# A hybrid decoder layer on one core: the delta rule's low-rank products change places with the first block of its input projections

## The chip, the core and the metric

The kernel runs on one core of a Trainium2 chip. The core has a matrix engine (TensorE, PE in the profile; PEld is its loading of weights), a vector engine (VectorE, DVE), a scalar engine (ScalarE, ACT), GpSimd (POOL) and a queue that only issues transfers (SyncE, SP). The metric is the device time of one execution in microseconds; lower is better.

## What is computed

One layer of a decoder trunk over 256 tokens of width 2048, in float32. Three token mixers (an mLSTM, an RWKV-7 delta rule, an S5 state space) read one combined projection of the normalised input. Their outputs are gated and merged, and a SwiGLU and a gated embedding follow. What this change touches is the front of the delta rule:

```python
z = xn @ w_in                      # columns: mLSTM | RWKV-7 | S5 | three gates
r, kr, vr, wl, al, gl = jnp.split(_token_shift(zr, mu), RWKV_SPLIT, axis=-1)
w = -softplus(-(w0 + jnp.tanh(wl) @ w2)) - 0.5     # w2: 96 x 512
a = sigmoid(a0 + al @ a2)                          # a2: 96 x 512
g = sigmoid(gl) @ g2                               # g2: 256 x 512
# r, kr, vr: 512 columns each; w, a, g enter the recurrence over 256 steps
```

Beside it in the program stands the S5 mixer: a complex diagonal recurrence, computed in eight slices of 2 x 128 states.

## The kernel before

**Weights.** Every weight matrix is cut into chunks of 512 x 512 (1 MB). The host lays them out one behind the other in the order of use (`layout`, array `wall`), and the kernel takes them strictly in that order: `load` issues the next chunk on SP into `raw` (a ring of three), `chunk` splits it, half a chunk at a time, into a high part `whi` (a cast on ACT, L124) and a low part `wlo` (a subtraction on DVE, L125). Each of these rings has three buffers of half a chunk. A product in full precision then takes three matmuls: high by high, high by low, low by high.

**Products.** A large product is a `gemm_fm` (weights stationary, L145, L146, L148) or a `gemm_tm` (activations stationary, L138, L139, L141). Each takes four chunks and two PSUM banks of the pool `mm`, which has four banks. `fm_small` (L131 to L133) is the small form; `lora` calls it three times on one chunk, with two banks each time and 12, 12 and 24 matmuls.

**The stages that the change touches.** `z_lora`, early in the program, computes the low-rank columns into `zpL`, which stays in SBUF. Much later `lora` makes the operands of the second product from it: the token shift into `lx` (ACT and DVE), tanh, then the split into `Lh` (a cast on ACT) and `Ll` (a subtraction on DVE); then it takes its chunk and runs the three small products, whose results ACT reads out into the tiles `lora`. `z_rkv(i)` for i = 0, 1, 2 computes r, k and v: a `gemm_fm`, read out of PSUM by DVE into `zp`, then a token shift on ACT and DVE into `mur`, `muk`, `muv`. `s5_slice(ip, jj)` begins with four matmuls on the tile `ub` (L489), then a long row of DVE work (`xr_`, `xi_`, `sr`, `si`, `wa`, `rr`), and every second slice a product with `cc` (L535). The tile `ub` has one buffer, which six transfers on POOL (L473, L474) refill for the next slice once the four matmuls have read it. The last part of the mLSTM, `ml_out`, scales `oth` on DVE and transposes it on PE (L356).

**Buffers.** `lx`, `Lh`, `Ll`, the three `lora` tiles, `zp`, `mur` and many others are tiles of 128 x 1024 from one pool (`t4`, 12 buffers). PSUM for the smaller products is the pool `sm` (four banks).

**What sets the order.** The order of the calls at the end of `trunk` is a wish: a scheduler orders the instructions of each engine when the program is built, by its own estimate of when each can run, with the earlier call in front where several can. `chunk` and the reading of PSUM have high priority. On the chip each engine's order is then fixed. The order of the calls and the order of the chunks in `wall` must agree, since chunks are taken in turn.

Of the kernel before, what the change touches and what calls it, by code (L numbers as in the profile page):

```python
# [70 lines left out]
def trunk(ctx: ExitStack, tc: tile.TileContext, xT, x, pT, wall, vecs, csts, s5b, s5c, gfin, out, dbg=None):  # L71
# [131 lines left out]
    def ts(o, i, a, b=None, op0=ALU.mult, op1=ALU.add):  # L203
        if b is None:
            nc.vector.tensor_scalar(out=o, in0=i, scalar1=a, scalar2=None, op0=op0)
        else:
            nc.vector.tensor_scalar(out=o, in0=i, scalar1=a, scalar2=b, op0=op0, op1=op1)
# [4 lines left out]
    def stt(o, a, s, b, op0, op1):  # L212
        nc.vector.scalar_tensor_tensor(out=o, in0=a, scalar=s, in1=b, op0=op0, op1=op1)
# [19 lines left out]
    def t8(name, dt=F32):  # L233
        return mp.tile([128, 8, T], dt, name=name, tag="b8", bufs=2)
# [116 lines left out]
    def tposed(src, n0):  # L351

        pt = psm()
        for a in range(2):
            for t in range(2):
                nc.tensor.transpose(pt[:, a * 256 + t * 128:a * 256 + (t + 1) * 128], src[t][:, (n0 + a) * 128:(n0 + a + 1) * 128], ident)  # L356
        return pt
# [346 lines left out]
    def ml_out():  # L704
        num, rh, oth = G["num"], G["rh"], G["o"]
        ymh, yml = t8("ymh", F32R), t8("yml", F32R)
        for t in range(2):
            stt(oth[t], oth[t], 1.0, num[t][:, :, 0:256], ALU.add, ALU.mult)
            for h in range(4):
                ts(oth[t][:, h, :], oth[t][:, h, :], rh[:, 4 * t + h:4 * t + h + 1])  # L710
        of = [o.rearrange("p h c -> p (h c)") for o in oth]
        for q in range(4):
            pt = tposed(of, 2 * q)
            for a in range(2):
                k = 2 * q + a
                split(ymh[:, k, :], yml[:, k, :], pt[:, a * 256:(a + 1) * 256], V("mng", k))
        G.update(ymh=ymh, yml=yml)
        dump("ymh", ymh.bitcast(F32))
        dump("yml", yml.bitcast(F32))
# [24 lines left out]
    def lora():  # L744
        zpL = G["zpL"]
        Lh = t4v(4, "Lh").bitcast(F32R)
        Ll = t4v(4, "Ll").bitcast(F32R)
        lx = t4v(4, "lx")
        for f in range(4):
            act_fn(lx[:, f, :], zpL[:, f, 1:257], AF.Identity, scale=omu(12 + f))  # L750
            stt(lx[:, f, :], zpL[:, f, 0:256], V("mul", f), lx[:, f, :], ALU.mult, ALU.add)
        act_fn(lx[:, 0, :], lx[:, 0, :], AF.Tanh)
        act_fn(lx[:, 2:4, :], lx[:, 2:4, :], AF.Tanh, scale=0.5)
        ts(lx[:, 2:4, :], lx[:, 2:4, :], 0.5, 0.5)
        split(Lh, Ll, lx)
        w = chunk()
        out_ = []
        for ks in ((0,), (1,), (2, 3)):
            rows = slice(0, 96) if ks[0] < 2 else slice(0, 128)
            ps = fm_small(w, ks, rows, lambda k: Lh[:, k, :], lambda k: Ll[:, k, :])  # L760
            o = t4v(4, "lora")
            for f in range(4):
                if ks[0] < 2:
                    i = 16 + 4 * ks[0] + f
                    act_fn(o[:, f, :], quarter(ps, f), AF.Tanh, scale=0.5, bias=vd[:, i:i + 1])
                else:
                    nc.scalar.copy(out=o[:, f, :], in_=quarter(ps, f))
            out_.append(o)
        G["lw"], G["aa"], G["gF"] = out_

    def z_rkv(i):
        mu = ("mur", "muk", "muv")[i]
        ps = gemm_fm(xh, xl, NKT)
        zp = t4("zp")[:, 0:1028].rearrange("p (a t) -> p a t", a=4)
        nc.vector.memset(zp[:, :, 0:1], 0.0)
        evac_fm(ps, zp, 1)
        o = t4v(4, mu)
        for f in range(4):
            act_fn(o[:, f, :], zp[:, f, 1:257], AF.Identity, scale=omu(4 * i + f))
            stt(o[:, f, :], zp[:, f, 0:256], V(mu, f), o[:, f, :], ALU.mult, ALU.add)  # L780
        G["rkv"[i] + "F"] = o
# [319 lines left out]
    ml_num()  # L1101
    z_o(1)
    ml_out()
    lora()
    z_rkv(0)
    s5_slice(1, 0)
    z_rkv(1)
    s5_slice(1, 1)
# [185 lines left out]
def layout(i):  # L1294

    f32 = np.float32
    a = {k: np.asarray(v) for k, v in i.items()}

    def fm(v):
        return np.ascontiguousarray(v.reshape(-1, 128).T)  # L1300

    def pad(v, n):
        o = np.zeros((n,), f32)
        o[:v.shape[0]] = v
        return o

    mu = a["rwkv_mu"][0]
    mul = np.concatenate([pad(mu[1536:1632], 128), pad(mu[1632:1728], 128), mu[1728:1984]])
    ifb = np.zeros((128, 2), f32)
    ifb[96:100, 0] = a["mlstm_ib"][0]  # L1310
    ifb[96:100, 1] = a["mlstm_fb"][0]
    ldt = np.ascontiguousarray(np.broadcast_to(a["s5_log_dt"][0][:, None], (32, 64)))
    parts = {
        "gmix": fm(a["norm_mix_g"][0]), "gffn": fm(a["norm_ffn_g"][0]), "gple": fm(a["norm_ple_g"][0]),
        "mng": fm(a["mlstm_norm_g"][0]), "conv": fm(a["mlstm_conv"][0]),
        "mur": fm(mu[0:512]), "muk": fm(mu[512:1024]), "muv": fm(mu[1024:1536]), "mul": fm(mul),
        "w0": fm(a["rwkv_w0"][0]), "a0": fm(a["rwkv_a0"][0]), "kk": fm(a["rwkv_kk"][0]), "ka": fm(a["rwkv_ka"][0]),
        "rk": fm(a["rwkv_rk"][0]), "lng": fm(a["rwkv_ln_g"][0]), "lnb": fm(a["rwkv_ln_b"][0]),
        "d": fm(a["s5_d"][0]), "glub": fm(a["s5_glu_b"][0]),
        "are": fm(a["s5_a_re"][0]), "aim": fm(a["s5_a_im"][0]), "ldt": fm(ldt), "ifb": ifb,  # L1320
    }
    vecs = np.concatenate([parts[n] for n, _ in VEC], axis=1)

    w_in = a["w_in"][0]
    z28 = np.zeros((D, 28), f32)
    lora_c = np.concatenate([w_in[:, 5640:5736], w_in[:, 4096:4100], z28, w_in[:, 5736:5832], w_in[:, 4100:4104], z28, w_in[:, 5832:6088]], axis=1)

    chunks = []

    def block(w):  # L1330
        k = w.shape[0]
        for c in range(k // 512):
            chunks.append(w[c * 512:(c + 1) * 512].reshape(4, 128, 512).transpose(1, 0, 2).reshape(128, 2048))

    def blocks(w):
        for n in range(w.shape[1] // 512):
            block(w[:, n * 512:(n + 1) * 512])

    block(w_in[:, 6088:6600])
    block(lora_c)  # L1340
    blocks(w_in[:, 0:4096])
    lw = np.zeros((4, 128, 512), f32)
    lw[0, :96] = a["rwkv_w2"][0]
    lw[1, :96] = a["rwkv_a2"][0]
    lw[2:4] = a["rwkv_g2"][0].reshape(2, 128, 512)
    block(lw.reshape(512, 512))
    blocks(w_in[:, 4104:5640])
    blocks(w_in[:, 6600:8648])
    block(a["s5_glu_w"][0])
    blocks(a["w_up_m"][0])  # L1350
    for n in range(4):
        block(w_in[:, 10696 + n * 512:10696 + (n + 1) * 512])
        block(a["w_up_s"][0][:, n * 512:(n + 1) * 512])
    blocks(w_in[:, 8648:10696])
    blocks(a["w_up_r"][0])
    blocks(a["w_out"][0])
    for n in range(11):
        block(a["ffn_w_gate"][0][:, n * 512:(n + 1) * 512])
        block(a["ffn_w_up"][0][:, n * 512:(n + 1) * 512])
    blocks(a["ffn_w_down"][0])  # L1360
    wp = a["ple_w_proj"][0]
    for n in range(4):
        if n % 2 == 0:
            block(np.concatenate([wp[:, n * 512:(n + 1) * 512], wp[:, (n + 1) * 512:(n + 2) * 512]], axis=0))
        block(a["ple_w_gate"][0][:, n * 512:(n + 1) * 512])
    wall = np.stack(chunks)

    s5b = np.zeros((128, 4, 2, 128), f32)
    s5c = np.zeros((128, 2, 16, 32), f32)
    for ri, (nb, ncn) in enumerate((("s5_b_re", "s5_c_re"), ("s5_b_im", "s5_c_im"))):  # L1370
        b, c = a[nb][0], a[ncn][0]
        for g in range(32):
            i_, jj, gg = g // 8, (g % 8) // 2, g % 2
            s5b[32 * jj + 16 * gg:32 * jj + 16 * gg + 16, i_, ri, 64 * gg:64 * gg + 64] = b[g].T
            s5c[64 * gg:64 * gg + 64, ri, g // 2, 16 * gg:16 * gg + 16] = c[g].T
    x2 = a["x"][0]
    return {
        "xT": np.ascontiguousarray(x2.T.reshape(16, 128, T).transpose(1, 0, 2)),
        "x": np.ascontiguousarray(x2),
        "pT": np.ascontiguousarray(a["p"][0, 0].T.reshape(2, 128, T).transpose(1, 0, 2)),  # L1380
        "wall": wall,
        "vecs": vecs,
        "csts": shape_constants(),
        "s5b": s5b,
        "s5c": s5c.reshape(128, 2, 512),
        "gfin": np.ascontiguousarray(a["final_norm_g"].reshape(1, D)),
    }
# [17 lines left out]
```

## Time and profile before

| | before |
|---|---|
| median of 3 runs | 1680.63 us (1679.04 to 1680.68) |
| the profiled execution, its own time | 1679.8 us |
| span of the profile (first to last instruction) | 1678.0 us |
| PE busy | 1658.7 us (99%) |
| DVE busy | 1059.9 us (63%) |
| ACT busy | 808.0 us (48%) |
| mean granted clock of TensorE | 0.998 of full speed |

The span is what the rows below are read from; the profiled execution took 1.8 us more than its span, and is 0.8 us under the median. A busy share is an average: what a stage is worth has to be read in that stage. Matmuls are pipelined, so the time from one start to the next says more than the duration of one.

### The profile page before, as it was taken

To read this page: it belongs to the slowest core of one execution; us is meant where nothing else is said; L and a number is where in the kernel's file an instruction comes from. 1 tells how busy PE (TensorE), PEld (TensorE's weight loads), DVE (VectorE), ACT (ScalarE), POOL (GpSimd) and SP (SyncE) were. 2 spreads that over 40 slices of the span, in tenths; PEclk is the share of its full clock that TensorE was granted. 3 is DMA by queue.
4 is the path that set the end of the run, shared out by engine and by line. 5 is a ranking of instruction groups with operands and counts; after the bars stand their busy time and mean duration, and the time that the engine had idled before them with its cause. 6 is when DMAs were issued, how large, how long until landed. Compare 5 with 4: busy or idle time off the path is not lost.

```text
span 1678.0 us, 22986 instructions
## 1 busy us (share of the span) xinstructions
PE 1658.7 (99%) x9354; PEld 1403.3 (84%) x9354; DVE 1059.9 (63%) x1330; ACT 808.0 (48%) x995; POOL 42.4 (3%) x65
## 2 busy tenths in 40 slices
PE   8999999999999999999999999999999999999997
PEld 8998889987888878888888888888888888888886
DVE  7999776968987555575555555555555545544565
ACT  6465566455555434444444444444444434444444
POOL 1100100100000000000000000000000000000000
PEclk9999999999999999999999999999999999999999
DMA  9654544555454444556555555555555555555553
GB/s 361 196 182 175 172 154 176 187 188 181 176 182 151 148 152 153 197 188 209 203 186 198 179 197 183 194 187 189 191 185 195 183 198 185 192 197 181 221 185 120
DMA packets 49450, 313.66 MB, mean 187 GB/s; under 512 B 5824, under 2 KB 9152, under 8 KB 12736
## 3 DMA queue, kind: packets, MB, share of 16 engines
q1 hardware_dynamic: 43488, 304.59, 50.7%
q0 software_dynamic: 3840, 3.15, 1.1%
q10 hardware_dynamic: 2016, 4.46, 0.8%
q8 instruction: 73, 1.20, 0.3%
q14 instruction: 33, 0.27, 0.0%
HBM read 306.93 MB, written 2.10 MB: 184 GB/s over the span
## 4 chain that ended last, share of the span: by engine, by line
PE 98%; ACT 1%; issue 1%; DMA 0%; DVE 0%; SPq 0%; POOLq 0%; POOL 0%
PE mm L138 26%; PE mm L139 26%; PE mm L141 26%; PE mm L145 4%; PE mm L146 4%; PE mm L148 4%; PE sm L535 1%; PE sm L1213 1%; PE mm L132 0%; PE mm L131 0%; PE mm L133 0%; PE sm L1158 0%; PE sm L878 0%; PE sm L356 0%; PE sm L1014 0%
## 5 line engine op out<-in xcount | busy, mean ns | idle before, releaser
L125 DVE TENSOR_TENSOR wlo<-raw,whi 128x1024 fp32r<-128x1024 f32 (+1 forms) x562 | 683.6, 1218 | 505.7 <-ACT whi L124 464.3
L124 ACT CAST whi<-raw 128x1024 fp32r<-128x1024 f32 (+1 forms) x562 | 589.1, 1049 | 788.1 <-PE mm L139 666.8
L138 PE MATMUL mm<-whi,hhi 128*128 128x512 f32 x704 | 274.1, 389 | 0.0
L139 PE MATMUL mm<-whi,hlo 128*128 128x512 f32 x704 | 274.0, 389 | 0.0
L139 PE MATMUL mm<-whi,alo 128*128 128x512 f32 x512 | 201.2, 393 | 0.0
L138 PE MATMUL mm<-whi,ahi 128*128 128x512 f32 x512 | 201.0, 393 | 0.0
L141 PE MATMUL mm<-wlo,hhi 128*128 128x512 f32 x704 | 193.5, 392 | 0.0
L139 PEld LDWEIGHTS mm<-whi,hlo 128*128 128x128 f32 x704 | 132.2, 188 | 27.6
L138 PEld LDWEIGHTS mm<-whi,hhi 128*128 128x128 f32 x704 | 132.2, 188 | 27.2
L141 PEld LDWEIGHTS mm<-wlo,hhi 128*128 128x128 f32 x704 | 132.2, 188 | 26.6
L145 PE MATMUL mm<-ahi,whi 128*128 128x256 f32 x576 | 143.2, 286 | 7.2 <-ACT whi L124 7.2
L146 PE MATMUL mm<-alo,whi 128*128 128x256 f32 x576 | 142.9, 285 | 0.0
L141 PE MATMUL mm<-wlo,ahi 128*128 128x512 f32 x512 | 139.3, 392 | 0.0
L138 PE MATMUL mm<-whi,gh 128*128 128x512 f32 x352 | 137.0, 389 | 0.0
L139 PE MATMUL mm<-whi,gl 128*128 128x512 f32 x352 | 137.0, 389 | 0.0
L145 PEld LDWEIGHTS mm<-ahi,whi 128*128 128x128 f32 x576 | 111.4, 194 | 8.0 <-ACT whi L124 7.2
L138 PEld LDWEIGHTS mm<-whi,ahi 128*128 128x128 f32 x512 | 96.1, 188 | 21.2 <-issue 1.2
L139 PEld LDWEIGHTS mm<-whi,alo 128*128 128x128 f32 x512 | 96.1, 188 | 21.0 <-issue 1.2
L141 PEld LDWEIGHTS mm<-wlo,ahi 128*128 128x128 f32 x512 | 95.6, 188 | 20.6 <-issue 0.4
L146 PEld LDWEIGHTS mm<-alo,whi 128*128 128x128 f32 x576 | 111.5, 194 | 0.4 <-issue 0.4
L141 PE MATMUL mm<-wlo,gh 128*128 128x512 f32 x352 | 96.0, 391 | 0.0
L148 PE MATMUL mm<-ahi,wlo 128*128 128x256 f32 x576 | 81.7, 284 | 0.0
(493 smaller groups left out, 1888.9 us busy)
## 6 DMA issues: line engine op xcount, KB each, us to landing
raw<-in_wall SPq DMA_DIRECT2D x283, 1024.0 KB, 4.8
xrow<-in_x SPq DMA_DIRECT2D x2, 1024.0 KB, 9.6
h<-in_x ACTq DMA_DIRECT2D x8, 256.0 KB, 3.3
xraw<-in_xT SPq DMA_DIRECT2D x3, 512.0 KB, 10.0
ub<-Bh POOLq DMA_DIRECT2D x16, 64.0 KB, 4.2
ub<-uh POOLq DMA_DIRECT2D x16, 64.0 KB, 4.4
gft<-in_gfin ACTq DMA_DIRECT2D x1, 1024.0 KB, 7.3
out_dram<-fin SPq DMA_DIRECT2D x4, 256.0 KB, 3.2
```

The costliest lines, as they stand in the source:

```text
L124: nc.scalar.copy(out=hi[:, q, :], in_=r)
L125: nc.vector.tensor_tensor(out=lo[:, q, :], in0=r, in1=hi[:, q, :].bitcast(F32), op=ALU.subtract)
L138: nc.tensor.matmul(ps, ah, wh, start=first, stop=False, skip_group_check=skip)
L139: nc.tensor.matmul(ps, al, wh, start=False, stop=False, skip_group_check=skip)
L141: nc.tensor.matmul(ps, ah, wl, start=False, stop=last, skip_group_check=skip)
L145: nc.tensor.matmul(ps, wh, ah, start=first, stop=False, skip_group_check=skip)
L146: nc.tensor.matmul(ps, wh, al, start=False, stop=False, skip_group_check=skip)
L148: nc.tensor.matmul(ps, wl, ah, start=False, stop=last, skip_group_check=skip)
L535: nc.tensor.matmul(psy[32 * j:32 * j + 32, a * 256:(a + 1) * 256], cc[:, ri, js_, :], G["s5x"][q][ri][:, a, :], start=ri == 0, stop=ri == ...
L1213: nc.tensor.transpose(pt[:, a * 256 + t * 128:a * 256 + (t + 1) * 128], sg[t][:, (2 * q + a) * 128:(2 * q + a + 1) * 128], ident)
```

## The change

In the list of calls, `lora()` moves behind `z_rkv(0)`, and in `layout` its chunk of weights moves behind the four chunks of `z_rkv(0)`:

```diff
     ml_num()
     z_o(1)
     ml_out()
+    z_rkv(0)
     lora()
-    z_rkv(0)
     s5_slice(1, 0)
     z_rkv(1)
...
     blocks(w_in[:, 0:4096])
+    blocks(w_in[:, 4104:4616])
     lw = np.zeros((4, 128, 512), f32)
...
     block(lw.reshape(512, 512))
-    blocks(w_in[:, 4104:5640])
+    blocks(w_in[:, 4616:5640])
     blocks(w_in[:, 6600:8648])
```

No instruction is added or removed. The scheduler, however, orders the neighbourhood anew, on three engines. In the rows of order below, the numbers are those of buffers.

**PE, where the three small products of `lora` begin.** Before, they stand right behind the last matmuls of `z_o(1)` (L141):

```order
L141 MATMUL mm_2564<-wlo_2675,ahi_82 128x512
L141 MATMUL mm_2565<-wlo_2675,ahi_82 128x512
L131 MATMUL mm_2778<-Lh_2752,whi_2770 128x256
L132 MATMUL mm_2778<-Ll_2753,whi_2770 128x256
L133 MATMUL mm_2778<-Lh_2752,wlo_2771 128x256
```

In the change they stand behind the last matmuls of `z_rkv(0)` (L148), with eight matmuls of S5 between (L489): four on `ub_2302`, which belong to `s5_slice(1, 0)`, and four on `ub_3101`, which belong to `s5_slice(1, 1)`:

```order
L148 MATMUL mm_2753<-ahi_82,wlo_2935 128x256 x2
L489 MATMUL sm_3095<-ub_2302 128x256
L489 MATMUL sm_3096<-ub_2302 128x256
L489 MATMUL sm_3095<-ub_2302 128x256
L489 MATMUL sm_3096<-ub_2302 128x256
L489 MATMUL sm_3392<-ub_3101 128x256
L489 MATMUL sm_3393<-ub_3101 128x256
L489 MATMUL sm_3392<-ub_3101 128x256
L489 MATMUL sm_3393<-ub_3101 128x256
L131 MATMUL mm_3025<-Lh_2999,whi_3017 128x256
```

Before, the four on `ub_3101` stood behind `z_rkv(1)`, a whole block of 192 matmuls after the four on `ub_2302`. Behind the first L131 of the change stand three more L131 and then the first L132, which reads `Ll`.

**ACT, where the operands of `lora` are made.** Before, the token shift `lx` stands among the casts of `z_o(1)`'s weights and the copies of `ml_num` (`num`, `jk`), far ahead of `z_rkv(0)`:

```order
L216 ACTIVATE oth_2359<-mm_2361,hrs0_398 128x512
L688 COPY num_2500<-sm_2504 128x258
L688 COPY num_2501<-sm_2510 128x258
L688 COPY num_2500<-sm_2517 128x258
L216 ACTIVATE lx_2754<-zpL_431,vd_140 128x256 x4
L216 ACTIVATE jk_2507,nss_2502<-num_2500 128x256
L124 CAST whi_2606<-raw_2600 128x1024
```

In the change it stands behind the cast for `z_rkv(1)`'s first weights, and behind the first two rows of `mur`, which read the result of `z_rkv(0)` from `zp`:

```order
L124 CAST whi_3149<-raw_3147 128x1024
L216 ACTIVATE mur_2990<-zp_2986,vd_140 128x256 x2
L216 ACTIVATE lx_3001<-zpL_431,vd_140 128x256 x4
L216 ACTIVATE mur_2990<-zp_2986,vd_140 128x256 x2
L216 ACTIVATE lx_3001<-lx_3001 128x256
L216 ACTIVATE lx_3001<-lx_3001 128x512
L184 CAST Lh_2999<-lx_3001 128x1024
```

**DVE, the same place.** Before, the three rows of `lora`'s operands stand between subtractions of weights (`wlo`), far ahead of `z_rkv(0)`:

```order
L213 SCALAR_TENSOR_TENSOR lx_2754<-zpL_431,vt_73,lx_2754 128x256 x4
L125 TENSOR_TENSOR wlo_2607<-raw_2600,whi_2606 128x1024
L207 TENSOR_SCALAR lx_2754<-lx_2754 128x512
L125 TENSOR_TENSOR wlo_2637<-raw_2634,whi_2636 128x1024
L185 TENSOR_TENSOR Ll_2753<-lx_2754,Lh_2752 128x1024
```

In the change they stand behind the reading of `z_rkv(0)`'s banks (two rows of `zp`, one `wlo`, then four rows of 128x512 that read `s5_slice(1, 0)`'s banks, all ahead of this piece) and among the rest of that slice's work:

```order
L213 SCALAR_TENSOR_TENSOR mur_2990<-zp_2986,vt_73,mur_2990 128x256 x2
L213 SCALAR_TENSOR_TENSOR lx_3001<-zpL_431,vt_73,lx_3001 128x256 x4
L213 SCALAR_TENSOR_TENSOR mur_2990<-zp_2986,vt_73,mur_2990 128x256 x2
L210 TENSOR_TENSOR xr__3125<-xr__3125,wa_3109 128x512
L210 TENSOR_TENSOR xi__3126<-xi__3126,rr_3108 128x512
L207 TENSOR_SCALAR lx_3001<-lx_3001 128x512
L519 SCALAR_TENSOR_TENSOR sr_3133<-s16mag_670,xr__3125 128x256 x2
L519 SCALAR_TENSOR_TENSOR si_3134<-s16mag_670,xi__3126 128x256 x2
L207 TENSOR_SCALAR wa_3406<-trow_663,s16f_681 128x256 x2
L210 TENSOR_TENSOR xr__3125<-sr_3133,tc_3110 128x512
L210 TENSOR_TENSOR rr_3108<-sr_3133,tsn_3111 128x512
L185 TENSOR_TENSOR Ll_3000<-lx_3001,Lh_2999 128x1024
```

What moved, beside the products: the making of their operands now begins behind `z_rkv(0)` instead of ahead of it. The rows of SP and POOL are in the same order in both programs.

## Rows read from the trace of the kernel before

**Rows 1.** The page: the span, and the chain that ended last.

```profile
span 1678.0 us, 22986 instructions
PE 98%; ACT 1%; issue 1%; DMA 0%; DVE 0%; SPq 0%; POOLq 0%; POOL 0%
```

**Rows 2.** PE's two longest waits: us in total, times, longest.

```profile
PE mm L145 <- ACT whi L124: 7.2, 1, 7.2
PE mm L131 <- ACT oth L216: 1.6, 1, 1.6
```

**Rows 3.** Timeline of PE through `lora`: start, us, instruction, count, idle before.

```profile
257.13 0.28 PE L131 MATMUL mm<-Lh,whi 96*128 96x256 f32 x1
...
260.25 0.41 PE L131 MATMUL mm<-Lh,whi 96*128 96x256 f32 x1 [1.59 <-ACT oth L216]
...
264.01 0.28 PE L131 MATMUL mm<-Lh,whi 128*128 128x256 f32 x1
...
266.05 0.28 PE L145 MATMUL mm<-ahi,whi 128*128 128x256 f32 x1
```

**Rows 4.** Windows of that stretch: busy PE, PEld, DVE, ACT, POOL, then PEclk.

```profile
257.00:258.70 1.70, 1.67 (x14) 1.43 (x12) 1.46 (x2) 1.68 (x3) 0.00 (x0) 1.00 0.00 0
262.00:263.00 1.00, 1.00 (x6) 1.00 (x6) 1.00 (x3) 1.00 (x4) 0.00 (x0) 0.50 0.14 57
```

**Rows 5.** Timeline of ACT and DVE: the operands of `lora` before.

```profile
235.38 1.74 ACT L216 ACTIVATE lx<-zpL,vd 128x256 f32<-128x256 f32 x4
239.42 0.93 ACT L216 ACTIVATE lx<-lx 128x256 f32<-128x256 f32 x2
242.49 1.05 ACT L184 CAST Lh<-lx 128x1024 fp32r<-128x1024 f32 x1
244.46 1.23 DVE L185 TENSOR_TENSOR Ll<-lx,Lh 128x1024 fp32r<-128x1024 f32 x1 [1.64 <-PE sm L685]
```

**Rows 6.** Timeline of PE and ACT at the end of `z_rkv(0)`.

```profile
290.80 0.64 PE L489 MATMUL sm<-ub 96*128 96x256 f32 x4
291.49 1.71 ACT L216 ACTIVATE mur<-zp,vd 128x256 f32<-128x256 f32 x4 [0.40 <-DVE zp L210]
```

**Rows 7.** Timeline of DVE from there on.

```profile
290.76 1.29 DVE L210 TENSOR_TENSOR zp<-mm,rsb 128x512 f32<-128x512 f32 x2 [1.30 <-PE mm L148]
291.97 1.22 DVE L125 TENSOR_TENSOR wlo<-raw,whi 128x1024 fp32r<-128x1024 f32 x1
293.10 0.68 DVE L210 TENSOR_TENSOR xr__3125<-sm,tc 128x512 f32<-128x512 f32 x1
...
295.50 0.47 DVE L213 SCALAR_TENSOR_TENSOR mur<-zp,vt,mur 128x256 f32<-128x256 f32 x1
...
297.09 1.21 DVE L125 TENSOR_TENSOR wlo<-raw,whi 128x1024 fp32r<-128x1024 f32 x1
...
300.56 1.26 DVE L519 TENSOR_TENSOR_SCAN sr<-s16mag,xr__3125 128x256 f32<-128x256 f32 x2
301.75 1.20 DVE L125 TENSOR_TENSOR wlo<-raw,whi 128x1024 fp32r<-128x1024 f32 x1
...
304.05 0.59 DVE L207 TENSOR_SCALAR wa<-trow,s16f 128x256 f32<-128x256 f32 x2
304.56 0.68 DVE L210 TENSOR_TENSOR xr__3125<-sr,tc 128x512 f32<-128x512 f32 x1
```

**Rows 8.** Instructions on `ub` from 290 to 300 us: duration in ns, starts; landing.

```profile
L474 POOL DMA_DIRECT2D ub<-ul x1: 537/537/537, 294.4 to 294.4; - x1
DMA to landing us min/median/max: 2.1/2.7/3.3
```

**Rows 9.** Window of that stretch, columns as in Rows 4.

```profile
291.30:305.60 14.30, 14.30 (x122) 14.30 (x121) 14.30 (x25) 6.60 (x9) 3.20 (x6) 1.00 0.61 198
```

**Rows 10.** Timeline of PE at the start of the program.

```profile
7.23 0.58 PE L145 MATMUL mm<-ahi,whi 128*128 128x256 f32 x1 [7.23 <-ACT whi L124]
...
10.59 0.41 PE L146 MATMUL mm<-alo,whi 128*128 128x256 f32 x1
```

## The prediction

> **What bounds the kernel now.** I read the page first. Nearly the whole chain that ended last is PE [rows 1]: a microsecond in which PE stands still is a microsecond of the result, and nothing on another engine counts unless PE waits for it. Next the waits of PE. The longest is the start of the program; the second is 1.6 us, inside `lora`, for ACT to read a bank that `z_o(1)` left [rows 2]. So the stage that the change moves is almost the only one in mid-program where PE loses time.
>
> Then that stage itself. `lora` takes from 257.13 to 266.05, 8.92 us for 48 matmuls [rows 3]. In its last part 18 matmuls go by from 264.01 to 266.05, 0.113 us each; 48 of them would be 5.44 us. The rest, 3.48 us, is two losses. The second product should begin 12 x 0.113 = 1.36 us after 257.13 and begins at 260.25: 1.76 us. And from 260.25 to 264.01 another 18 matmuls take 3.76 us in place of 2.04: 1.72 us. There the granted clock is 0.50, the 1.2 GHz level, after 1.00 ahead of the gap [rows 4]. A gap of 1.6 us was enough here for PE to come back at half clock.
>
> Last, when the operands of `lora` are ready. `Ll`, the last of them, is made at 244.46 and takes 1.23 us [rows 5], over 11 us ahead of its first use. Today nothing of their making lies on the path.
>
> **The change part by part.**
>
> *Removed.* Both losses of 1.76 and 1.72 us. The wait was for ACT, which reads `z_o(1)`'s banks late behind other work; in the new place the second product uses banks that DVE empties at the head of its queue. Bounds for this gain: nothing, if a wait of the same kind comes back, to 3.48 us. I take all of it, since the banks are empty long before the new products can start.
>
> *The same.* All 48 matmuls, the chunk's four casts and four-part split, and its load on SP. In SP's queue one load changes places with four, each load still goes out when a buffer of `raw` comes free, and POOL's order is untouched: nothing for these. `z_rkv(0)` starts 8.92 us earlier. Its operand `ahi` is there, its first three half chunks are cast during `z_o(1)` as `lora`'s are now, and its banks are the pair that `z_o(0)` left long ago: nothing.
>
> *Moved: the operands.* This is the term that decides. In the new order ACT comes to `lx` only behind two rows of `mur`, which need `zp`, which DVE can only read once `z_rkv(0)` has finished. So the whole making of `Lh` and `Ll` now begins when PE has run out of `z_rkv(0)`, and PE has little to do meanwhile. I price it by the same instructions in today's trace, taking the end of `z_rkv(0)` there, 290.80, as zero hour [rows 6]. DVE's queue, from 290.76, by the steps from start to start [rows 7]:
>
> - two readings into `zp`: 291.97 - 290.76 = 1.21; one `wlo`: 293.10 - 291.97 = 1.13;
> - four rows of 128x512: 295.50 - 293.10 = 2.40, so 0.60 each;
> - eight rows of 128x256 (`mur`, `lx`, `mur`): four took 297.09 - 295.50 = 1.59, so 3.18;
> - `xr` and `xi`: 1.20; `lx`, 128x512: priced as `wa` of the same size, 304.56 - 304.05 = 0.51;
> - the scans `sr` and `si`: 301.75 - 300.56 = 1.19 each, 2.38; `wa`: 0.51; `xr` and `rr`: 1.20.
>
> That is 13.72, so `Ll` starts at 304.48, and with its 1.23 it is there at 305.71, 14.9 us after zero hour.
>
> Is anything later than DVE's queue? ACT does `mur` from 291.49 [rows 6]; eight such rows at 1.74 / 4 = 0.44 [rows 5] give `lx` by 294.1, and DVE asks for it at 296.3. DVE is through `lx` at 297.9; two tanh take 0.93 [rows 5], to 298.8, and DVE comes to the next step at 299.9. Then `Lh` from 300.4, 1.05, ready at 301.5; DVE comes to `Ll` only at 304.5. So it is DVE's queue, with S5's rows ahead of `Ll`, that sets the end, with 3 us to spare. The second four L489 want a refill of `ub`: the last of its six transfers is issued at 294.4 and lands at most 3.3 us later [rows 8], at 297.7. That also lies inside.
>
> In these 14.9 us PE has eight L489 and four L131, twelve matmuls at 0.113: 1.4 us. The other 13.5 us it waits. Behind the waiting L132 stand the remaining 44 matmuls of `lora` and all of `z_rkv(1)`; ACT's next cast waits for a `whi` buffer that `lora` holds, and SP's loads behind that. All of them shift together, so the wait costs its length once.
>
> *Bounds of that term.* If each of DVE's rows costs its duration in place of its step, the sum is 16.6 (1.29, 1.22, 4 x 0.68, 8 x 0.47, 2 x 0.68, 0.59, 2 x 1.26, 0.59, 2 x 0.68, 1.23), and the wait 15.2. Below I see no reason for less than 13.4. I take 13.5, since DVE stood in today's trace in just such a row of work.
>
> *The clock.* After a gap of 1.6 us PE came back at half clock and lost 1.72 us [rows 3, 4]; after the 7.23 us at the start it steps by about 0.21 us too, to 10.59 and beyond [rows 10]. I take 1.72 again. Bounds: nothing, and half clock through all 44 matmuls, 44 x 1.72 / 18 = 4.2.
>
> *What comes next.* The third product takes the banks of the first, read by four rows of ACT (1.7 us) while the second's matmuls run (some 2 us at half clock); `z_rkv(1)` takes the second's, read during the third's 24 matmuls. I take nothing; at most a microsecond.
>
> *The sum.* +13.5 + 1.72 - 1.76 - 1.72 = +11.7 us. Against the profiled execution, 1679.8, that is 1691.5. The median of before lies 0.8 us above that execution, so I predict **1692.3 us**. By the bounds: 13.4 - 3.5 = +9.9 gives 1690.5; 15.2 + 4.2 + 1 - 3.5 = +16.9 gives 1697.5.
>
> **A rule weighed against a row.** The six transfers into `ub` come from POOL's queue. In today's trace they landed in 2.1 to 3.3 us [rows 8] while DVE was busy 14.30 of 14.30 us [rows 9], so a busy DVE didn't hold them. The Trainium skill (SBUF — State Buffer, section "SBUF: two separate sides") warns that GpSimd can't write the descriptors of its transfers while DVE runs an op in a two-port fast mode, and that the transfer then seems stuck behind DVE. By the row the refill costs nothing in the sum; by the rule it would be the third rival below. The trace speaks against it in the very stretch concerned.
>
> **The rivals.**
>
> *The change only gains (other side of no change).* If the operands were ready when `z_rkv(0)` ends, the two losses would go and nothing come: 1680.6 - 3.5 = 1677.1. The point that decides is how late `Ll` is: ready within 1.4 + 3.5 = 4.9 us of the end, the change still doesn't lose. For it: `zpL` is there from early on, and today DVE and ACT make the operands between other rows [rows 5]. Against it: in the new order ACT's `lx` stands behind `mur`, and DVE's seven rows ahead of its first `mur` alone are 1.21 + 1.13 + 2.40 = 4.7 us. Chance 0.03.
>
> *Longer behind the gap.* PE stays at half clock through `lora`, and the reading of banks on ACT falls behind the products. For it: PE starts and stops in the gap three times (L489, L489, L131). Against it: it recovered after 3.8 us today [rows 3]. Time: 1692.3 + 2.5 + 1 = 1695.8. Chance 0.10.
>
> *The refill of `ub` waits for DVE to pause.* After `Ll` DVE has eight more instructions (four of 0.60, one of 0.51, three of 0.40, 4.1 us) before one needs a result of `lora`; the refill would land 2.7 us after that [rows 8], at 312.5 in place of inside the gap, 6.8 us later: 1699.1. Against it: rows 8 and 9. Chance 0.05.
>
> *The change does nothing.* DVE gets S5's rows done during the gap, and if PE had later waits for DVE, they would shrink by as much. But its waits behind `lora` are all under 1.6 us [rows 2] and the chain that ended last is 98% PE [rows 1]: there is nothing to give back. Chance 0.02.
>
> **How the numbers follow.** The forecast has the remaining 0.80, at 1692.3, by its bounds 1690.5 to 1697.5, most of it low in them. The range 1689.5 to 1697 holds it but for its last half microsecond, and the second rival; left out are the first, third and fourth, 0.10 together, and the tails. About 0.2%, 3.4 us, is what a measurement of this kernel can tell from no change. Faster is the first rival, 0.03; within 0.2% the last, 0.02; slower the other three, 0.95.
>
> **What would show it.** In the profile after: one wait of PE in front of L132, released by DVE's `Ll`, and before it idle times in front of the second four L489 (ended by a transfer) and of L131 (ended by ACT's `Lh`), about 13.5 us together; no wait for `oth` in `lora`; `z_rkv(0)` from 257 to 282; DVE busy without a pause from there to `Ll`; granted clock 0.50 for some 3 to 4 us behind the gap; DVE's and ACT's busy sums unchanged. I would be wrong if `lx` ran during `z_rkv(0)`, if a transfer into `ub` ended the gap, or if PE showed new waits later on.

## The result and the profile after

The changed kernel takes 1693.97 us (median of 6 runs, 1691.54 to 1695.04), the kernel before 1680.66 us in the same comparison (1679.04 to 1680.79): 1.008 times the time, with a 95% interval of 1.007 to 1.009. The forecast was 1692.3 us with a range of 1689.5 to 1697. The profiled execution took 1694.65 us. Of all the executions below, one of e1's twelve took 3290.96 us, about twice the others, and stands outside e1's interval.

| | after |
|---|---|
| span of the profile | 1692.9 us |
| PE busy | 1663.4 us (98%) |
| DVE busy | 1061.0 us (63%) |
| ACT busy | 809.2 us (48%) |
| mean granted clock | 0.993 |

DVE and ACT do the same work as before. PE is busy 4.7 us more with the same matmuls: that is, in the main, time at half clock. The rest of the 14.9 us by which the span grew is standing still. From the page of the changed kernel, the span and the chain that ended last:

```profile
span 1692.9 us, 22989 instructions
PE 97%; DVE 1%; issue 1%; ACT 0%; DMA 0%; SPq 0%; POOLq 0%; POOL 0%
```

PE's waits in the changed kernel (us in total, times, longest), to be laid beside [rows 2]:

```profile
PE mm L145 <- ACT whi L124: 7.4, 1, 7.4
PE sm L489 <- DMA ub<-ul: 5.5, 1, 5.5
PE mm L131 <- ACT Lh L184: 3.3, 1, 3.3
PE mm L132 <- DVE Ll L185: 2.9, 1, 2.9
```

The wait of 1.6 us for `oth` is gone. Three new ones have come, 11.7 us together. The timeline of PE shows that they are one stop in three pieces:

```profile
283.88 0.64 PE L489 MATMUL sm<-ub 96*128 96x256 f32 x4
290.01 1.19 PE L489 MATMUL sm<-ub 96*128 96x256 f32 x4 [5.49 <-DMA ub<-ul]
294.49 1.22 PE L131 MATMUL mm<-Lh,whi 96*128 96x256 f32 x4 [3.29 <-ACT Lh L184]
298.61 0.58 PE L132 MATMUL mm<-Ll,whi 96*128 96x256 f32 x1 [2.89 <-DVE Ll L185]
...
305.61 0.29 PE L132 MATMUL mm<-Ll,whi 128*128 128x256 f32 x1
```

`z_rkv(0)` ends where the first L489 begins, at 283.88. The first product that needs `Ll` runs at 298.61, 14.73 us later. What DVE does in that time, from its timeline:

```profile
283.84 1.29 DVE L210 TENSOR_TENSOR zp<-mm,rsb 128x512 f32<-128x512 f32 x2 [1.29 <-PE mm L148]
...
286.18 0.69 DVE L210 TENSOR_TENSOR xr__3125<-sm,tc 128x512 f32<-128x512 f32 x1
...
289.36 1.67 DVE L213 SCALAR_TENSOR_TENSOR lx<-zpL,vt,lx 128x256 f32<-128x256 f32 x4
...
293.27 1.27 DVE L519 TENSOR_TENSOR_SCAN sr<-s16mag,xr__3125 128x256 f32<-128x256 f32 x2
...
297.33 1.22 DVE L185 TENSOR_TENSOR Ll<-lx,Lh 128x1024 fp32r<-128x1024 f32 x1
```

and from ACT's, the only other row on which `Ll` rests:

```profile
293.39 1.05 ACT L184 CAST Lh<-lx 128x1024 fp32r<-128x1024 f32 x1 [1.71 <-DVE lx L207]
```

`Lh` is there at 294.44, yet DVE takes up `Ll` only at 297.33, behind the scans and four more rows of S5. Windows of the changed kernel (busy PE, PEld, DVE, ACT, POOL, then the granted clock): the stop, the products behind it, what follows, and a stretch early in the program to which the last section comes back:

```profile
283.84:298.55 14.71, 3.10 (x14) 2.33 (x12) 14.71 (x28) 5.72 (x12) 6.34 (x12) 0.66 0.46 122
298.60:305.40 6.80, 6.79 (x27) 5.76 (x28) 6.14 (x12) 4.83 (x10) 0.00 (x0) 0.50 0.00 0
306.00:310.00 4.00, 4.00 (x37) 4.00 (x35) 0.00 (x1) 3.21 (x6) 0.00 (x0) 1.00 0.73 262
165.00:169.00 4.00, 4.00 (x11) 2.93 (x10) 2.91 (x6) 0.00 (x0) 0.00 (x0) 0.58 0.70 262
```

DVE is busy 14.71 of 14.71 us, PE 3.10. Behind the stop PE works without a pause at the 1.2 GHz level until about 305.5, then at full clock. Nothing of the loss is given back later: at the first matmul of L878, far behind the stage, the changed kernel is 14.80 us late (519.75 against 504.95), and 14.84 at the end.

The 14.84 us lie in two places. From the first matmul behind `z_o(1)` (257.13 before, 259.11 in the change) to the last instruction the change takes 1433.76 us in place of 1420.89: 12.87 us more. This time, from the end of `z_o(1)` on, is used again below. The other 1.97 us come ahead of that point: 0.40 us before the first L635 (163.01 and 163.41), and 1.58 us between there and the end of `z_o(1)`, by a half clock at 165 us that the last section takes up.

### The profile page after: what moved, and what is told of

It is laid out like the page before. It is cut to its first block, busy times and chain, and to the rows that moved or that the text cites. A ratio compares the mean times of both kernels' runs of the same rounds, so it can differ in the third digit from the quotient of the medians.

```text
span 1692.9 us, 22989 instructions
## 1 busy us (share of the span) xinstructions
PE 1663.4 (98%) x9354; PEld 1407.1 (83%) x9354; DVE 1061.0 (63%) x1330; ACT 809.2 (48%) x995; POOL 42.4 (3%) x65
## 4 chain that ended last, share of the span: by engine, by line
PE 97%; DVE 1%; issue 1%; ACT 0%; DMA 0%; SPq 0%; POOLq 0%; POOL 0%
PE mm L138 26%; PE mm L139 26%; PE mm L141 26%; PE mm L145 4%; PE mm L148 4%; PE mm L146 4%; PE sm L535 1%; PE sm L1213 1%; PE mm L132 1%; PE mm L133 0%; PE mm L131 0%; PE sm L1158 0%; PE sm L878 0%; PE sm L356 0%; DMA raw<-in_wall 0%
## 5 line engine op out<-in xcount | busy, mean ns | idle before, releaser
L138 PE MATMUL mm<-whi,hhi 128*128 128x512 f32 x704 | 274.1, 389 | 0.0
L138 PE MATMUL mm<-whi,ahi 128*128 128x512 f32 x512 | 201.7, 394 | 0.0
L141 PE MATMUL mm<-wlo,hhi 128*128 128x512 f32 x704 | 193.5, 392 | 0.0
L138 PEld LDWEIGHTS mm<-whi,hhi 128*128 128x128 f32 x704 | 132.2, 188 | 27.2
L141 PEld LDWEIGHTS mm<-wlo,hhi 128*128 128x128 f32 x704 | 132.2, 188 | 26.6
L141 PE MATMUL mm<-wlo,ahi 128*128 128x512 f32 x512 | 139.8, 393 | 0.0
L138 PE MATMUL mm<-whi,gh 128*128 128x512 f32 x352 | 137.0, 389 | 0.0
L138 PEld LDWEIGHTS mm<-whi,ahi 128*128 128x128 f32 x512 | 96.6, 189 | 21.0 <-issue 0.8
L141 PEld LDWEIGHTS mm<-wlo,ahi 128*128 128x128 f32 x512 | 95.9, 188 | 20.6 <-issue 0.4
L141 PE MATMUL mm<-wlo,gh 128*128 128x512 f32 x352 | 96.0, 391 | 0.0
L148 PE MATMUL mm<-ahi,wlo 128*128 128x256 f32 x576 | 81.6, 285 | 0.0
```

Source lines behind the costliest of these rows:

```text
L138: nc.tensor.matmul(ps, ah, wh, start=first, stop=False, skip_group_check=skip)
L141: nc.tensor.matmul(ps, ah, wl, start=False, stop=last, skip_group_check=skip)
L148: nc.tensor.matmul(ps, wl, ah, start=False, stop=last, skip_group_check=skip)
```

## The experiments

**The theory.** The time goes because the operands of `lora` are made only behind `z_rkv(0)`, and on DVE behind S5's rows: PE stands still for them, and comes back at half clock. **The rivals.** The place of the products or of their chunk costs the time itself; or the refill of `ub`, which the first and longest wait names; or the half clock belongs to the products and not to the stop. "Us" below is the median; before was 1680.23 us for the first four kernels and 1680.36 us for the next two.

| kernel | us | to before, 95% interval | PE's waits in the stage, us |
|---|---|---|---|
| e1, operands early | 1677.07 | 0.9984 (0.9975 to 0.9993) | none |
| e2, two buffers for `ub` | 1695.92 | 1.0091 (1.0078 to 1.0104) | 9.5, 2.9 |
| e3, S5 behind the operands | 1687.01 | 1.0041 (1.0028 to 1.0054) | 6.9 |
| e4, one block further on | 1691.55 | 1.0068 (1.0055 to 1.0081) | 5.4, 3.9, 1.0 |
| e5, 56 extra matmuls | 1690.85 | 1.0067 (1.0052 to 1.0082) | none |
| e6, 34 extra matmuls | 1685.23 | 1.0034 (1.0020 to 1.0048) | none |

**e1: the products moved, the operands not.** `lora` is cut in two, and only its second half stands behind the block. The order of the chunks is that of the change.

```diff
         split(Lh, Ll, lx)
+        G["Lh"], G["Ll"] = Lh, Ll
+
+    def lora_mm():
+        Lh, Ll = G["Lh"], G["Ll"]
         w = chunk()
...
-    z_rkv(0)
     lora()
+    z_rkv(0)
+    lora_mm()
     s5_slice(1, 0)
```

> The low-rank products and their chunk of weights stay behind the first block of the projections, as in the changed kernel, but their operands lx, Lh and Ll are written out ahead of that block, as in the kernel before. Theory (the time goes because TensorE waits for these operands, which VectorE and ScalarE reach only behind the block's own rows): the waits of 5.5, 3.3 and 2.9 us and the half clock behind them are gone, the 1.59 us wait of the kernel before and its half clock too, so 1677 to 1679 us, up to 1680 if a small wait for a bank is left. Rival (the place of the products or of the chunk of weights itself costs the time): 1690 us or more.

1677.07 us, 3.16 us under before. All of PE's waits in its profile:

```profile
PE mm L145 <- ACT whi L124: 7.2, 1, 7.2
PE mm L138 <- ACT gate L216: 0.6, 1, 0.6
PE mm L138 <- ACT whi L124: 0.2, 1, 0.2
```

Neither the new wait nor the old one for `oth` is left. The chunk and the products stand where the change put them, and the kernel is a little faster than before, by less than the 0.2% named ahead but with an interval that leaves out no change. So the place of products and chunk costs nothing; the whole loss of the change, 1693.97 against 1677.07, comes with the operands. This holds in the profiles too: from the end of `z_o(1)` on, e1 takes 1417.34 us, 16.4 less than the change and 3.55 less than before. This is the version that beats both kernels.

**e2: a second buffer for `ub`.** The longest wait in the changed kernel is the one for a transfer into `ub`.

```diff
-    b2 = ctx.enter_context(tc.tile_pool(name="b2", bufs=16))
+    b2 = ctx.enter_context(tc.tile_pool(name="b2", bufs=14))
...
-        ub = pa.tile([96, 2, 512], F32R, name="ub", tag="ub")
+        ub = pa.tile([96, 2, 512], F32R, name="ub", tag="ub", bufs=2)
```

> The changed kernel with two buffers for ub in place of one, and two fewer in pool b2 to make room. Theory (all three waits are one wait for Ll, which is as late as before): the 5.5 us wait of the second group at L489 for its transfer is gone, and the waits at L131 and L132 grow by as much, so 1693 to 1695 us. Rival (the single buffer of ub costs its own 5.5 us): about 1688.5 us.

1695.92 us, a microsecond above what the theory named, and seven above the rival. PE's waits:

```profile
PE mm L131 <- ACT Lh L184: 9.5, 1, 9.5
PE mm L145 <- ACT whi L124: 6.9, 1, 6.9
PE mm L132 <- DVE Ll L185: 2.9, 1, 2.9
```

The wait for the transfer is gone, and L131's is longer by 6.2 us: 12.4 us in place of 11.7. The stop is as long as it was, 298.72 - 283.99 = 14.73 us:

```profile
283.99 1.12 PE L489 MATMUL sm<-ub 96*128 96x256 f32 x8
298.72 0.58 PE L132 MATMUL mm<-Ll,whi 96*128 96x256 f32 x1 [2.90 <-DVE Ll L185]
```

So the row of 5.5 us was only the first event that PE met in a stop that ends with `Ll`. Part of the microsecond too much is a wait that the changed kernel has not, 0.6 us at L138 for DVE's `gate`; whether it comes from the smaller pool `b2` was not tried.

**e3: S5's rows behind the operands.** One matmul more, which reads `Lh`, whose result nothing uses:

```diff
         split(Lh, Ll, lx)
         w = chunk()
+        nc.tensor.matmul(psm(), Lh[:, 0, 0:128], w[0][0], start=True, stop=True)
```

It makes the scheduler write S5's rows behind `Ll` on DVE.

> The changed kernel with one extra matmul, whose result nothing uses, that reads Lh ahead of the products. It changes the order in which the rows are laid out: the S5 stage's rows on VectorE then stand behind Ll and its small matmuls at L489 behind the first products. Theory (Ll is late by what VectorE has in front of it): Ll comes about 8.3 us after the block's last matmul in place of 14.7, so the time falls by about 6 us to 1687 to 1688 us. Rival (the chain from the block through lx and Lh sets the delay, S5's rows only fill it): no change, 1693 to 1695 us.

1687.01 us. From its profile, PE's wait in this place (L757 is the extra matmul) and the row of `Ll` in DVE's timeline:

```profile
PE sm L757 <- ACT Lh L184: 6.9, 1, 6.9
```

```profile
290.56 1.23 DVE L185 TENSOR_TENSOR Ll<-lx,Lh 128x1024 fp32r<-128x1024 f32 x1 [1.11 <-ACT Lh L184]
```

`z_rkv(0)` ends at 283.7 here, so `Ll` is there 8.1 us later in place of 14.7. The time fell by 7.0 us: a little under half of the delay is S5's rows in front of `Ll`. The rest is the chain from `zp` through `mur` and `lx` to `Lh`, in which DVE now waits for ACT (1.11 us).

**e4: one block further on.** The products and their chunk behind `z_rkv(1)`, shown against the changed kernel:

```diff
     z_rkv(0)
-    lora()
     s5_slice(1, 0)
     z_rkv(1)
+    lora()
...
-    blocks(w_in[:, 4104:4616])
+    blocks(w_in[:, 4104:5128])
...
-    blocks(w_in[:, 4616:5640])
+    blocks(w_in[:, 5128:5640])
```

> The products and their chunk of weights one block further on, behind the second block of the projections. Theory (whichever block they stand behind, the operands come behind that block's evacuation): a wait of 8 to 12 us in front of the products again, so 1689 to 1693 us. Rival (the place behind the first block is special, by what S5 does there): no wait of over 2 us, 1677 to 1681 us.

1691.55 us. PE's waits:

```profile
PE sm L489 <- DMA ub<-ul: 5.4, 1, 5.4
PE mm L131 <- ACT Lh L184: 3.9, 1, 3.9
PE mm L132 <- DVE Ll L185: 1.0, 1, 1.0
```

The same three, 10.3 us, now behind `z_rkv(1)`. The first block is not special; behind either of the two blocks that were tried, the operands are written behind its read-out.

**e5 and e6: is the half clock the stop's or the products'?** Extra matmuls of 128x512 ahead of the products, whose result nothing uses, so that PE works while it would wait: 56 in e5, as shown, and 34 in e6. They change the order too: the scheduler puts S5's rows on DVE behind `Ll`, as in e3.

```diff
         w = chunk()
+        pf = psm()
+        for _ in range(56):
+            nc.tensor.matmul(pf, ahi[:, 0, 0:128], w[0][0], start=True, stop=True)
```

> The changed kernel with 56 extra matmuls of 128x512, whose result nothing uses, between the block and the products, so that TensorE works through the wait: at 0.227 us each that is 12.7 us. Theory (the half clock behind the wait comes from the idle engine, and costs the changed kernel about 3.6 us on top of its waits): the granted clock stays 1.00 through the products and the time is that of the kernel with early operands plus the fill, 1677.1 + 12.7 = 1689.8 us. Rival (the clock is halved for the products themselves, whatever stands ahead of them): 1692 to 1694 us.

> The same with 34 extra matmuls, 7.7 us, which is about as long as the operands take when S5's rows stand behind Ll on VectorE. Theory: no wait of over 1 us ahead of the products, a clock of 1.00, and 1677.1 + 7.8 = 1684.9 us, up to 1685.5. Rival (the clock is halved for the products whatever stands ahead): 1687 us or more.

1690.85 us for e5, a microsecond above the theory's number and one below the rival's range; 1685.23 us for e6, in the theory's range. The traces decide. First e5, then e6, windows of the extra matmuls and of the products, columns as above:

```profile
283.00:295.60 12.60, 12.60 (x58) 10.43 (x57) 7.08 (x13) 5.56 (x12) 0.00 (x0) 1.00 0.19 79
295.60:301.80 6.20, 6.20 (x54) 6.16 (x53) 3.42 (x6) 4.63 (x11) 2.34 (x5) 1.00 0.13 23
```

```profile
282.37:290.00 7.63, 7.63 (x36) 6.28 (x35) 6.51 (x13) 5.43 (x12) 0.00 (x0) 1.00 0.32 129
290.00:296.00 6.00, 6.00 (x53) 6.00 (x52) 5.93 (x11) 4.31 (x11) 3.19 (x6) 1.00 0.38 67
```

The clock is 1.00 through the products in both. In the changed kernel and in e3, where PE stands still ahead of them, it is 0.50 when they begin. The window of e3 is

```profile
290.60:294.80 4.20, 4.20 (x18) 4.10 (x19) 3.08 (x5) 0.61 (x2) 1.42 (x3) 0.50 0.08 16
```

So it is the stop that halves it, and not the products. With useless matmuls in the stop e6 is 1.8 us faster than e3, whose DVE has the same order and whose PE stands still for 6.9 us. The lone half clock at 165 us, which e3's profile has and e6's has not, is of that size, but it stands ahead of the end of `z_o(1)`: from there on e3 takes 1426.95 us and e6 1425.35, 1.60 less. By the same measure e5 takes 1430.26 us and the early operands 1417.61 (e7): the fill costs e5 12.65 us and e6 7.74, which are their 56 and 34 matmuls at 0.227 us (12.7 and 7.7), to a tenth. So e5's profile shows nothing in this stage of the microsecond that its median lies too high, but a late start: the first L635 comes at 164.07 us, in e7 at 162.83.

**Second profiles of three kernels (e7, e8, e9).** One execution each, to see what comes back.

> A second profiled execution of the kernel with early operands. Theory (the half clock at 165 to 169 us comes in some executions and not in others, and is worth 1.5 us): the execution is near 1676.7 us with a clock of 1.00 there, or near 1678.3 us with 0.5 there. Rival (the two have nothing to do with each other): a time near 1676.7 us with a clock of 0.5 there, or 1678.3 us with 1.00.

> A second profiled execution of the kernel before. Theory (the half clock at 165 to 169 us has nothing to do with the change): it can show here too; an execution near 1680.5 us would show it, one near 1678.6 us not. Rival (it comes with the change's order): 1.00 in every execution of this kernel.

> A second profiled execution of the changed kernel. Theory: the three waits add up to 11 to 12 us again and the clock is 0.50 from about 290 to 305 us again, since these come from the order of the operands; the half clock at 165 to 169 us may be there (near 1694.7 us) or not (near 1692.5 us). Rival (the half clock behind the waits is as much a matter of chance as the one at 165 us): a clock of 1.00 at 299 to 305 us, and about 1690 us.

e7, the early operands again: 1676.38 us, and a clock of 1.00 where the first had 0.57 (1678.06 us). Windows of the first and of the second execution:

```profile
165.00:169.00 4.00, 4.00 (x12) 3.03 (x11) 2.91 (x6) 0.00 (x0) 0.00 (x0) 0.57 0.69 262
```

```profile
165.00:169.00 4.00, 4.00 (x19) 3.02 (x18) 2.67 (x6) 1.16 (x2) 0.00 (x0) 1.00 0.66 252
```

Two executions of one program, 1.68 us apart in time and 1.7 us in span: the theory's pairs. The half clock itself is 1.58 us of that: from the first L635 to the end of `z_o(1)` the first execution takes 95.71 us, the second 94.13. e9, the changed kernel again: 1694.39 us, waits of 5.4, 3.4 and 2.9 us, 0.50 behind them and a low clock at 165 to 169 us, as the first time; so the half clock behind the long stop was there in both. e8, the kernel before again: 1678.79 us and no low clock at 165 us, which leaves open whether this kernel can show it (the theory needed an execution near 1680.5 us); and a surprise in the stage of [rows 3, 4]. PE's wait and the window behind it:

```profile
PE mm L131 <- ACT oth L216: 1.6, 1, 1.6
```

```profile
260.00:264.00 4.00, 3.07 (x26) 3.07 (x27) 3.22 (x7) 3.99 (x10) 0.00 (x0) 1.00 0.61 246
```

The wait of 1.6 us is there again, and the clock stays at 1.00 behind it. From the end of `z_o(1)` on this execution takes 1419.22 us, 1.67 less than the first.

## Why the prediction was right, point by point

- **Removed, 1.76 us.** Right: no wait for `oth` is left in the changed kernel.
- **Removed, 1.72 us of half clock.** Only partly right. It was read from one execution; in the second one of the same kernel it was not there, and that one was 1.67 us shorter from there on. Behind a gap of 1.6 us the clock was halved in one execution of two.
- **The operands decide, `Ll` 14.9 us after the end of `z_rkv(0)`.** Right, and by the named mechanism: 14.73 us, with DVE busy in all of it and S5's rows ahead of `Ll`. e1 shows that without this delay nothing is lost (1677.07 us, where the first rival named 1677.1 for operands that are ready in time), e3 that S5's rows are a little under half of it. The steps inside were good to a microsecond: `Lh` was forecast for 10.7 us and came at 10.56 (294.44 - 283.88); the refill of `ub` for 6.9 us, and the second four L489 ran at 6.13.
- **13.5 us of it waited.** The three waits are 11.7 us. The twelve small matmuls were priced at full clock, 1.4 us. The first four took the 0.64 us of [rows 6], but the other eight ran at half clock (0.50 from 290.36 to 291.00 and from 294.40 to 295.70), 1.19 and 1.22 us for each four. PE is busy 3.10 us in the stop, and that shortens its waits and not the stop.
- **The clock behind the stop, 1.72 us.** This is the term that was mis-sized. From 298.61 to 305.61 PE runs 28 matmuls in 7.00 us, where "some 3 to 4 us" of half clock were forecast. The same 28 at full clock are 3.55 us (24 products at 0.115 as in e1, two L535 in 0.55 and two L489 in 0.24 as in the kernel before), so 3.45 us are lost. "I take 1.72 again" carried a price from a gap of 1.6 us to a stop of 14.7; the bounds, up to 4.2, held it. The rival of the longer half clock was right that it lasts longer, though it held for 24 of the remaining 44 products and not for all, and wrong that ACT's reading of banks would follow: no such wait is in the profile. The measured median lies about midway between the forecast, 1692.3, and this rival's 1695.8.
- **The refill of `ub`.** No term of its own, as forecast: e2 took the wait away and gained nothing. In the changed kernel POOL issued the refills for `ub` while DVE was busy without a pause. From issue to landing the twelve transfers into `ub` between 283 and 295 us took

```profile
DMA to landing us min/median/max: 1.9/2.1/3.1
```

  By the rule in the Trainium skill (SBUF — State Buffer, section "SBUF: two separate sides"), GpSimd can't write the descriptors of its transfers while DVE runs an op in a two-port fast mode. A refill held in this way until DVE paused would have landed behind 298.55, and the second four L489 run at 290.01. So DVE's rows here did not hold these transfers. The profile doesn't say which of the rows ran in such a mode, so this neither bears the rule out nor refutes it.
- **Nothing given back, nothing new later.** Right: PE has no other new wait.
- **The sum.** For the stage: 14.73 less the twelve small matmuls, 1.4, plus 3.5 of clock, less 1.76 and 1.72, is 13.35 us. The profiles show 12.87 us from the end of `z_o(1)` on, against a forecast of 11.7; where the half microsecond between 13.35 and 12.87 lies was not traced. The profiled executions differ by 14.85, since that of the changed kernel has the 1.58 us of half clock at 165 us as well, which the forecast could not contain, and comes 0.40 us later to that place. That the medians differ by 13.3, so near the sum, may be in part chance: profiled executions of one kernel differ in whether a lone half clock came, and in their start.

Not settled: why the scheduler writes `lx` behind `mur`, when `zpL` is ready long before. No experiment took that up.

## What to carry to other kernels

When a product is moved behind another block, look where its operands go: here they were written out with it, and ended up behind the read-out of the very block that was to be put in front. Move the product and leave its operands where they are, as e1 does. And a wait row names what PE met first, not what ends the stop: here the last of three waits in a row decided, and taking the first away only lengthened the next.

## What the runs showed of the hardware beside this

The granted clock is not the same in every execution of one program. Behind eight matmuls of 4 rows (L635), and with PE busy without a gap, it fell to between 0.57 and 0.64 on the mean of 165 to 169 us in five of the eleven profiled executions (the changed kernel twice, e1, e2, e3), and was 1.00 in the other six (before twice, e4 to e7); the instructions there are the same in all. It is worth 1.58 us: from the first L635 to the end of `z_o(1)` the five take 95.70 to 95.71 us, the six 94.12 to 94.13. The half clock behind the 1.6 us wait in the kernel before came in one execution of two. What decides it is open. The start varies too: the first L635 came between 162.83 and 164.07 us. A term of this size is read from more than one profile.
